# A hybrid encoder's mixer: the convolution's passes at a step's end, a norm factor on GpSimd, and squares between the parts of the head

## The chip, the cores and the metric

The kernel runs on one core of one Trainium2 chip. The metric is the time of the whole program on the device in microseconds (us), as the median of three runs. The engines are named as in the profile: PE is TensorE, DVE is VectorE, ACT is ScalarE, POOL is GpSimd and SP is SyncE, which only issues DMAs here.

## The reference

The input is x, 512 tokens of 1024 numbers. Each of two layers adds to x the output of a mixer and then of a mixture of experts. What matters here is the mixer, which is cut to its core (h is the normalised x):

```python
proj = rmsnorm(x, norm_mix[l]) @ w_in[l]
q, k, v, gate_b, gate_c, u = split(proj)             # 512, 128, 128, 512, 512, 512 wide
y_attn = windowed_gqa_with_sink(rope(q), rope(k), v, sink)   # 8 heads of 64, |i - j| <= 128
cu = gate_c * u
y_conv = gate_b * (cu[t-1] * w[0] + cu[t] * w[1] + cu[t+1] * w[2])
y = concat([rmsnorm(y_attn, g_attn), rmsnorm(y_conv, g_conv)])
x = x + y @ w_out[l]
```

Because the norm of x has one factor r per token, the projections can be made of x times the norm's weights alone, and r is multiplied in behind. The product gate_c * u then needs r squared for each token. The product with gate_b gets its one r within the norm of y_conv.

## The kernel before, in words

A mixer has three parts. In the **head**, 512 tokens of x are transposed on TensorE (parts T), copied out of PSUM as a high part by ACT and a low part by DVE (parts H), multiplied by the norm's weights. Every projection is made of high and low parts, three matmuls for each, so that the result is as exact as f32. The strings `HEAD` (layer 0) and `HEAD1` (layer 1) are the order of the head's parts, read by `stage`: f brings the end of the layer before, w splits a weight chunk, P makes a projection. Behind the head come **steps**. In step n a projection of 128 channels by 512 tokens is made on TensorE (8 parts, P in the string `STEP`), and the result of step n - 1 is taken over by `take`; FT lists whose projection it is: k, v, q (four pairs of heads), u, c (gate_c) and b (gate_b), of which the last three come four times each, and a u is followed by a c and the c by a b of the same 128 channels. Between the projection's parts the attention of a unit (one pair of heads and one block of 128 queries) is worked on:

```python
STEP = "P P K P S s T0 e T1 t1 n P R t0 w P P V v P P"
```

S is the scores on TensorE, s (`greatest`, L653) the maximum on DVE, e (`exps`) the exponentials on ACT, n (`normalise`, L671 to L674) the sum, the reciprocal and the scaling on DVE. T and t transpose the probabilities and split them (L410 on ACT, L411 on DVE), V and v multiply by the values. K calls `take`, R runs what is queued in `pend`, w splits the next weight chunk (L410, L411), and `post` runs at the end of the step. The last part are the **output** groups: y is split (L413 on ACT, L414 on DVE), multiplied by w_out, which GpSimd splits (`osplit`), and each result is added to x on DVE (L815) which frees its bank.

The names around the change: `rsv` holds the mean of squares per token, its rstd and the square of the rstd, in three rows. `sq_row` is r squared as a row of 512 tokens, the same in all partitions. In `take`, u is copied out of PSUM by ACT (L575), and multiplied by sq_row on DVE (L577); a c step multiplies the PSUM projection by u on DVE (L583), scales it by the middle weight on ACT (L584), and adds the two shifted terms in two passes on DVE (L585, L586). A b step multiplies that by its projection (L589), and `sums` adds up squares on ACT and GpSimd. `squares` (L481) is called at R of step 1 and makes the sums of squares of x by four ACT instructions, followed by the power on GpSimd.

What sets the order on each engine: TensorE and GpSimd are in program order (PINNED is "TG"). In the steps, DVE and ACT instructions are put in order when the program is built, by a planner's estimates of when each can start; in the head all three compute orders are those of the program. Tiles named t_N come from pools, and N is a count.

## Time and profile before

| What | us |
|---|---|
| median of three runs | 1368.87 |
| the three runs | 1370.92, 1368.45, 1368.87 |
| the profiled execution, its time | 1370.96 |
| the profiled execution, its span | 1369.2 |
| TensorE busy in the span | 1308.7 (96%) |
| DVE busy | 613.1 (45%) |
| ACT busy | 375.3 (27%) |
| POOL busy | 110.2 (8%) |

The time of an execution is from its start to its end as the device counts it, and the span is from the first to the last instruction in the trace. Busy shares are means over all stages. The mixers take 0 to 205 and 670 to 880 us; the experts lie between and behind them.

### The profile page before, as it was taken

Reading aid. Unit: us, or ns where it says so; the run is one execution under the profiler, and the core shown is the slowest. Engines: PE = TensorE matmul, PEld = TensorE weight load, DVE = VectorE, ACT = ScalarE, POOL = GpSimd, SP = SyncE. Lnnn points to the kernel's source line nnn. Section 1 sums busy time; section 2 is a strip of 40 time slices with the busy share of each in tenths; the row PEclk is TensorE's granted clock in tenths of the full one; section 3 lists DMA queues with packets and bytes.
Section 4 is the critical chain, followed back from the end, with each engine's and each line's share of the span. In section 5 each row is a group of like instructions: output and inputs, shape, how many; then the busy total and the mean of one; then the engine's idle time right before and its main releaser. Section 6 shows DMA issues by size and latency. Waiting matters only on the chain. (4 is left out here: it accounts for less than half of the span.)

```text
span 1369.2 us, 22469 instructions
## 1 busy us (share of the span) xinstructions
PE 1308.7 (96%) x8036; PEld 770.8 (56%) x8036; DVE 613.1 (45%) x1519; ACT 375.3 (27%) x819; POOL 110.2 (8%) x119
## 2 busy tenths in 40 slices
PE   9999899999999999999989998999999999999997
PEld 8777787445444355444377886865444443544442
DVE  4888745232344224222268888352334442332232
ACT  5565531221111111111156665212311011111112
POOL 1201340000000000000030023300000000000001
PEclk9999899999999999999999999999999999999999
DMA  8622267899999999999891223788999999999996
GB/s 257 189 65 75 93 261 278 344 377 419 419 418 419 419 419 419 418 419 419 329 280 50 67 75 130 263 329 343 378 418 419 419 418 419 419 419 419 418 418 253
DMA packets 160853, 438.47 MB, mean 320 GB/s; under 512 B 19352, under 2 KB 56672, under 8 KB 160736
## 3 DMA queue, kind: packets, MB, share of 16 engines
q1 hardware_dynamic: 160736, 436.98, 81.9%
q8 instruction: 65, 1.06, 0.3%
q14 instruction: 52, 0.43, 0.1%
HBM read 434.83 MB, written 2.10 MB: 319 GB/s over the span
## 5 line engine op out<-in xcount | busy, mean ns | idle before, releaser
L180 PE MATMUL A<-t,t 128*32 128x512 f32 (+3 forms) x3832 | 692.0, 527 | 12.3 <-DMA t<-in_w_expert_up_dram 2.5
L180 PEld LDWEIGHTS A<-t,t 128*32 128x32 f32 (+2 forms) x3832 | 334.4, 142 | 326.6 <-issue 235.9
L180 PE MATMUL C<-t,t 128*32 128x512 f32 (+4 forms) x1448 | 227.1, 569 | 4.0 <-DVE t L552 2.3
L180 PEld LDWEIGHTS C<-t,t 128*32 128x32 f32 (+2 forms) x1448 | 83.8, 126 | 132.0 <-issue 112.8
L414 DVE SCALAR_TENSOR_TENSOR t<-C,tg,t 128x512 fp32r<-128x512 f32 x56 | 41.3, 749 | 195.9 <-ACT t L413 194.5
L180 PE MATMUL B<-t,t 128*128 128x256 f32 (+3 forms) x836 | 112.0, 284 | 6.8 <-DVE t L1238 4.7
L1313 DVE SCALAR_TENSOR_TENSOR t<-A,tg,t 128x512 f32<-128x512 f32 x28 | 21.0, 751 | 213.6 <-PE A L180 197.1
L180 PEld LDWEIGHTS B<-t,t 128*128 128x128 f32 (+1 forms) x836 | 103.7, 186 | 22.5 <-issue 9.2
L180 PE MATMUL D<-t,t 128*128 128x512 f32 (+1 forms) x374 | 99.8, 366 | 10.9 <-DVE x L1344 6.3
L1344 DVE TENSOR_TENSOR x<-x,D 128x512 f32<-128x512 f32 x104 | 71.2, 685 | 77.6 <-PE D L180 77.3
L1312 ACT ACTIVATE t<-A,tg 128x512 f32<-128x512 f32 x28 | 19.3, 688 | 301.8 <-PE A L180 279.8
L413 ACT ACTIVATE t<-C,tg 128x512 fp32r<-128x512 f32 x56 | 37.8, 687 | 194.3 <-PE C L180 194.3
L180 POOL TENSOR_TENSOR t<-t,t 128x512 f32<-128x512 f32 (+1 forms) x34 | 61.2, 1801 | 213.1 <-ACT t L602 86.8
L1253 ACT ACTIVATE t<-B,gf 128x256 f32<-128x256 f32 (+1 forms) x96 | 38.4, 454 | 140.9 <-PE B L180 125.0
L180 PEld LDWEIGHTS D<-t,t 128*128 128x128 f32 x374 | 54.2, 179 | 39.7 <-DVE x L1344 13.1
L180 PE MATMUL F<-t,t 128*128 128x512 f32 x214 | 71.6, 414 | 0.1
L1344 DVE TENSOR_TENSOR x<-x,F 128x512 f32<-128x512 f32 x104 | 70.7, 680 | 0.0
L180 PE MATMUL B<-cst,t 128*128 128x128 f32 (+1 forms) x332 | 49.6, 274 | 14.0 <-DVE t L674 10.5
L180 PEld LDWEIGHTS B<-cst,t 128*128 128x128 f32 (+1 forms) x332 | 41.3, 151 | 24.7 <-issue 18.4
L180 PEld LDWEIGHTS F<-t,t 128*128 128x128 f32 x214 | 37.1, 188 | 18.9 <-DVE x L1344 11.4
L410 ACT ACTIVATE t<-t 128x1024 fp32r<-128x1024 f32 x44 | 45.8, 1054 | 0.1
L1215 DVE TENSOR_SCALAR t<-cst,sq 128x256 fp32r<-128x256 f32 (+1 forms) x64 | 17.2, 332 | 59.7 <-PE A L180 45.1
(278 smaller groups left out, 1059.2 us busy)
## 6 DMA issues: line engine op xcount, KB each, us to landing
t<-in_w_expert_gate_dram SPq DMA_DIRECT2D x256, 512.0 KB, 9.9
t<-in_w_expert_up_dram SPq DMA_DIRECT2D x256, 512.0 KB, 9.9
t<-in_w_expert_down_dram SPq DMA_DIRECT2D x256, 512.0 KB, 9.9
t<-in_w_in_dram SPq DMA_DIRECT2D x36, 512.0 KB, 6.4
t<-in_w_out_dram SPq DMA_DIRECT2D x16, 512.0 KB, 3.7
x<-in_x_dram SPq DMA_DIRECT2D x4, 512.0 KB
out_dram<-t SPq DMA_DIRECT2D x3, 512.0 KB, 2.7
t<-in_consts_dram SPq DMA_DIRECT2D x2, 512.0 KB
```

What stands on the lines that cost most here:

```text
L180: return (lambda *args, **kw: self.tc.keep_in_program_order(fn(*args, **kw))) if self.pinned else fn
L410: A.activation(hi, src, AF.Copy)
L413: A.activation(hi, src, AF.Copy, scale=scale)
L414: V.scalar_tensor_tensor(lo, src, scale, f(hi), op0=OP.mult, op1=OP.subtract)
L1215: V.tensor_scalar(oh[:, t, :w], io, sq[:, 0, t:t + 1], None, op0=OP.is_equal)
L1253: A.activation(hg[b][c // 4][:, c % 4 + cc, :w], p[:, cc, :w], AF.Copy, scale=g_ffn[:, c + cc:c + cc + 1])
L1312: A.activation(a, pg, AF.Silu, scale=rs)
L1313: V.scalar_tensor_tensor(a, pu, rs, a, op0=OP.mult, op1=OP.mult)
L1344: V.tensor_add(x[:, t, s], x[:, t, s], p)
```

## The change

Three things are moved. The four squares of x become stages c0 to c3 of the head, written between its parts, with a fresh junk tile for each; c3 also issues the power and the square of the rstd. The multiplication by `sq_row` leaves u (L577) and becomes a GpSimd instruction on the product of c and u, between DVE's product and ACT's scaling. And the two passes on DVE go into `post`, which runs at the end of the step.

```diff
--- before.py
+++ after.py
@@ -155,10 +155,10 @@
 PINNED = "TG"
 
 
-HEAD = ("z40 T00 T01 T02 T03 z08 T10 H00 T11 H01 T12 w0 H02 T13 H03 w1 z16 P00 T20 T30 H10 T21 T31 H11 T22 T32 H12 T23 T33 "
-        "H13 P01 P10 P11")
-HEAD1 = ("f0 f1 f2 w0 T00 T10 H00 T01 T11 H01 f3 T02 T12 H02 T03 T13 H03 w1 P00 T20 T30 H10 T21 T31 H11 P10 "
-         "T22 T32 H12 T23 T33 H13 P01 P11")
+HEAD = ("z40 T00 T01 T02 T03 z08 T10 H00 T11 H01 T12 w0 H02 T13 H03 w1 c0 c1 z16 P00 T20 T30 H10 T21 T31 H11 T22 T32 H12 T23 T33 "
+        "H13 c2 c3 P01 P10 P11")
+HEAD1 = ("f0 f1 f2 w0 T00 T10 H00 T01 T11 H01 f3 T02 T12 H02 T03 T13 H03 w1 c0 P00 T20 T30 H10 c1 T21 T31 H11 c2 P10 "
+         "T22 T32 H12 c3 T23 T33 H13 P01 P11")
 TURNS = ["BBCCDFBB", "BBBBCCBB"]
 
 AHEAD = [2, 3]
@@ -470,17 +470,15 @@
                 if a not in pp:
                     pp[a] = ps("A")
                 proj(a, pp[a], 0, ND, slice(b * 256, b * 256 + 256))
+            elif what == "c":
+                A.activation(t2([P, D], BF16), x[:, a], AF.Square, scale=D ** -0.5, accum_out=rsv[:, 0, a:a + 1])
+                if a == NT - 1:
+                    rstd_of(rsv[:, 0], rsv[:, 1])
+                    GP.tensor_mul(rsv[:, 2], rsv[:, 1], rsv[:, 1])
             else:
                 z = ps("D", (P, P))
                 for _ in range(10 * a + b):
                     T.matmul(z, onesb, onesb, start=True, stop=True)
-
-        def squares():
-            junk = t2([P, D], BF16)
-            for t in range(NT):
-                A.activation(junk, x[:, t], AF.Square, scale=D ** -0.5, accum_out=rsv[:, 0, t:t + 1])
-            rstd_of(rsv[:, 0], rsv[:, 1])
-            GP.tensor_mul(rsv[:, 2], rsv[:, 1], rsv[:, 1])
 
         for what in (HEAD, HEAD1)[l].split():
             stage(what[0], int(what[1]), int((what + "0")[2]))
@@ -573,17 +571,16 @@
             elif what[0] == "u":
                 st["u"] = t2([P, S])
                 A.activation(st["u"], p, AF.Copy)
-                u = st["u"]
-                post.append(lambda: V.tensor_mul(u, u, sq_row))
             elif what[0] == "c":
                 cu = t4([P, S + 2])
                 GP.memset(cu[:, 0:1], 0.0)
                 GP.memset(cu[:, S + 1:S + 2], 0.0)
                 c, v = what[1], st["u"]
                 V.tensor_mul(cu[:, 1:S + 1], p, v)
+                GP.tensor_mul(cu[:, 1:S + 1], cu[:, 1:S + 1], sq_row)
                 A.activation(v, cu[:, 1:S + 1], AF.Copy, scale=cw[:, 1, c:c + 1])
-                V.scalar_tensor_tensor(v, cu[:, 0:S], cw[:, 0, c:c + 1], v, op0=OP.mult, op1=OP.add)
-                V.scalar_tensor_tensor(v, cu[:, 2:S + 2], cw[:, 2, c:c + 1], v, op0=OP.mult, op1=OP.add)
+                post.append(lambda: [V.scalar_tensor_tensor(v, cu[:, n:S + n], cw[:, n, c:c + 1], v, op0=OP.mult, op1=OP.add)
+                                     for n in (0, 2)])
             else:
                 c = what[1]
                 V.tensor_mul(yc[c // 2][:, c % 2], p, st["u"])
@@ -731,8 +728,6 @@
                 elif m == "R" and n == 2:
 
                     flush(2)
-                elif m == "R" and n == 1:
-                    squares()
                 elif m == "w":
                     ahead()
                 elif m in "Ssen" and a:
```

The order of VectorE (DVE) in layer 0's first u step, from the sum of the denominators (L671 before, L668 of the changed kernel) to the maximum of the next unit (L653, L650, the rows ISA). t_858 is u, t_91 holds the mask and sq_row, nb the denominators, t_777 and t_780 the probabilities; before:

```order
L671 TENSOR_TENSOR nb<-nb 128x2
L710 TENSOR_TENSOR t_412<-D,yl 64x128
L577 TENSOR_TENSOR t_858<-t_858,t_91 128x512
L672 RECIPROCAL nb<-nb 128x2
L710 TENSOR_TENSOR t_412<-D,yl 64x128
L653 ISA t_864,nb<-C,t_91,sink 128x256
L653 ISA nb 128x1
L674 TENSOR_SCALAR t_777<-t_777,nb 128x256 x2
L653 ISA t_864,nb<-C,t_91,sink 128x256
```

and of the changed kernel:

```order
L668 TENSOR_TENSOR nb<-nb 128x2
L707 TENSOR_TENSOR t_423<-D,yl 64x128
L669 RECIPROCAL nb<-nb 128x2
L671 TENSOR_SCALAR t_780<-t_780,nb 128x256 x2
L707 TENSOR_TENSOR t_423<-D,yl 64x128
L650 ISA t_867,nb<-C,t_91,sink 128x256
L650 ISA nb 128x1
```

The product L577 is gone, and the normalisation (L674, now L671) stands ahead of both maxima and not between them.

The order of ScalarE (ACT) at the end of the head of layer 1; the rows with rsv are squares of x, those with gx are the copies out of the transposes, and t_6205 and t_6219 are split weights; before:

```order
L180 ACTIVATE t_5979<-B,gx 128x256 x2
L180 ACTIVATE t_5980<-B,gx 128x256 x2
L180 ACTIVATE t_6205<-t_5925 128x1024
L528 ACTIVATE t_6211<-A 128x512
L481 ACTIVATE t_6214,rsv<-x 128x1024 x2
L569 ACTIVATE t_6235<-A 128x512
L481 ACTIVATE t_6214,rsv<-x 128x1024 x2
L180 ACTIVATE t_6222<-t_5935 128x1024
```

and of the changed kernel:

```order
L180 ACTIVATE t_6065,rsv<-x 128x1024
L180 ACTIVATE t_5980<-C,gx 128x256 x2
L180 ACTIVATE t_6101,rsv<-x 128x1024
L180 ACTIVATE t_5981<-C,gx 128x256 x2
L180 ACTIVATE t_6112,rsv<-x 128x1024
L180 ACTIVATE t_5982<-B,gx 128x256 x2
L180 ACTIVATE t_6148,rsv<-x 128x1024
L180 ACTIVATE t_5983<-B,gx 128x256 x2
L180 ACTIVATE t_6219<-t_5928 128x1024
L526 ACTIVATE t_6225<-A 128x512
L180 ACTIVATE t_6228<-t_5938 128x1024
L567 ACTIVATE t_6241<-A 128x512
```

The squares stood behind the copies, around the projections' copies (L528, L569), and now one stands ahead of each pair of copies.

The order of VectorE (DVE) in the step of layer 0's fourth c, from the product of c and u (L583 before, L579 of the changed kernel; t_1508 and t_1511 are u and then the sum of the passes) to the splits of the gated product (L414); before:

```order
L583 TENSOR_TENSOR t_1586<-A,t_1508 128x512
L653 ISA t_1597,nb<-C,t_91,sink 128x384
L653 ISA nb 128x1
L585 SCALAR_TENSOR_TENSOR t_1508<-t_1586,prm,t_1508 128x512
L653 ISA t_1597,nb<-C,t_91,sink 128x384
L653 ISA nb 128x1
L411 TENSOR_TENSOR t_1609<-B,t_1608 128x256 x2
L586 SCALAR_TENSOR_TENSOR t_1508<-t_1586,prm,t_1508 128x512
L655 TENSOR_SCALAR nb<-nb 128x2
L414 SCALAR_TENSOR_TENSOR t_1643<-t_410,prm,t_1642 128x512
```

and of the changed kernel:

```order
L579 TENSOR_TENSOR t_1588<-A,t_1511 128x512
L650 ISA t_1598,nb<-C,t_91,sink 128x384
L650 ISA nb 128x1
L650 ISA t_1598,nb<-C,t_91,sink 128x384
L650 ISA nb 128x1
L411 TENSOR_TENSOR t_1610<-B,t_1609 128x256
L652 TENSOR_SCALAR nb<-nb 128x2
L411 TENSOR_TENSOR t_1610<-B,t_1609 128x256
L653 TENSOR_TENSOR nb<-sink,nb 128x2
L582 SCALAR_TENSOR_TENSOR t_1511<-t_1588,prm,t_1511 128x512 x2
L668 TENSOR_TENSOR nb<-nb 128x2
L586 TENSOR_TENSOR t_422<-A,t_1511 128x512
```

The two passes (L585 and L586, now two rows L582) stood apart from each other between the maxima, and now stand together behind the splits of B (L411).

## Rows read from the trace of the kernel before

**Rows 1.** The page's line of busy time, share of the span and instructions, and the trace's windows over the two mixers: length in us, then busy us of PE, PEld, DVE, ACT and POOL (with instructions), granted clock, DMA share and GB/s.

```profile
PE 1308.7 (96%) x8036; PEld 770.8 (56%) x8036; DVE 613.1 (45%) x1519; ACT 375.3 (27%) x819; POOL 110.2 (8%) x119
...
0.00:205.00 205.00, 191.45 (x1031) 161.97 (x1032) 146.44 (x362) 108.75 (x249) 48.31 (x45) 0.98 0.48 157
...
670.00:880.00 210.00, 194.39 (x1043) 156.96 (x1043) 147.31 (x355) 111.34 (x252) 51.01 (x42) 0.99 0.45 147
```

**Rows 2.** TensorE's timeline at the passes behind the normalisation of the three u steps of layer 0 and of the first two of layer 1. Columns here and in the groups of timelines below: start us, us, engine, line, operation, out<-in, shape, count, and in brackets idle time before and its releaser.

```profile
73.97 0.67 PE L180 MATMUL B<-cst,t 128*128 128x128 f32 x4 [1.09 <-DVE t L674]
...
105.11 0.67 PE L180 MATMUL B<-cst,t 128*128 128x128 f32 x4 [1.13 <-DVE t L674]
...
135.38 0.67 PE L180 MATMUL B<-cst,t 128*128 128x128 f32 x4 [1.14 <-DVE t L674]
...
750.78 0.67 PE L180 MATMUL B<-cst,t 128*128 128x128 f32 x4 [1.10 <-DVE t L674]
...
781.22 0.68 PE L180 MATMUL B<-cst,t 128*128 128x128 f32 x4 [1.09 <-DVE t L674]
```

**Rows 3.** VectorE's timeline in layer 0's first u step.

```profile
71.97 0.67 DVE L577 TENSOR_TENSOR t<-t,t 128x512 f32<-128x512 f32 x1
...
73.07 0.48 DVE L653 CUSTOM_DVE_ANT_0 t<-C,t,sink 128x256 f32<-128x256 f32 x1
...
73.48 0.61 DVE L674 TENSOR_SCALAR t<-t,nb 128x256 f32<-128x256 f32 x2
```

**Rows 4.** The timeline of GpSimd, VectorE and TensorE where the first query's rotation ends, in layer 0 and then in layer 1.

```profile
38.51 1.27 POOL L180 TENSOR_TENSOR t<-t,t 128x512 f32<-128x512 f32 x1
...
39.54 0.78 DVE L577 TENSOR_TENSOR t<-t,t 128x512 f32<-128x512 f32 x1
...
42.45 0.47 PE L180 MATMUL C<-t,t 128*128 128x256 f32 x2 [0.37 <-DVE t L552]
...
715.95 1.29 POOL L180 TENSOR_TENSOR t<-t,t 128x512 f32<-128x512 f32 x1
...
716.76 1.02 DVE L577 TENSOR_TENSOR t<-t,t 128x512 f32<-128x512 f32 x1 [0.90 <-ACT t L575]
...
719.92 0.47 PE L180 MATMUL C<-t,t 128*128 128x256 f32 x2 [1.60 <-DVE t L552]
```

**Rows 5.** The head of layer 1: TensorE's wait, ScalarE's last copies out of the transposes, the last square, and GpSimd's power.

```profile
705.66 0.82 PE L180 MATMUL C<-cst,rsv 128*128 128x128 f32 x5 [1.60 <-POOL rsv L180]
...
695.16 0.84 ACT L180 ACTIVATE t<-B,gx 128x256 fp32r<-128x256 f32 x2 [2.78 <-PE B L180]
...
703.01 1.06 ACT L481 ACTIVATE t<-x 128x1024 bf16<-128x1024 f32 x1
...
704.56 1.04 POOL L180 TENSOR_TENSOR rsv<-rsv,mhalf 128x4 f32<-128x4 f32 x1
```

**Rows 6.** ScalarE's timeline in the head of layer 0, the copies out of the transposes behind its idle time.

```profile
15.29 0.84 ACT L180 ACTIVATE t<-D,gx 128x256 fp32r<-128x256 f32 x2 [2.00 <-PE D L180]
```

**Rows 7.** Layer 0's first c step: ScalarE's scaling, VectorE's first pass and its splits of B, TensorE's wait for them.

```profile
49.51 0.72 ACT L584 ACTIVATE t<-t,prm 128x512 f32<-128x512 f32 x1 [1.68 <-DVE t L583]
...
50.33 0.75 DVE L585 SCALAR_TENSOR_TENSOR t<-t,prm,t 128x512 f32<-128x512 f32 x1 [0.86 <-ACT t L584]
...
52.74 0.75 DVE L411 TENSOR_TENSOR t<-B,t 128x256 fp32r<-128x256 f32 x2
...
53.54 0.57 PE L180 MATMUL D<-t,t 128*64 128x256 f32 x3 [1.17 <-DVE t L411]
```

**Rows 8.** VectorE's and GpSimd's timelines, instructions of these two engines beside each other and apart.

```profile
56.65 0.75 DVE L674 TENSOR_SCALAR t<-t,nb 128x384 f32<-128x384 f32 x2
...
86.84 1.83 DVE L674 TENSOR_SCALAR t<-t,nb 128x384 f32<-128x384 f32 x2
...
87.17 1.29 POOL L180 TENSOR_TENSOR t<-t,t 128x512 f32<-128x512 f32 x1 [16.61 <-ACT t L602]
...
64.56 1.79 POOL L180 TENSOR_TENSOR t<-t,t 128x512 f32<-128x512 f32 x1 [24.72 <-DVE t L531]
...
142.76 0.61 DVE L653 CUSTOM_DVE_ANT_0 t<-C,t,sink 128x384 f32<-128x384 f32 x1
...
142.94 1.30 POOL L180 TENSOR_TENSOR t<-t,t 128x512 f32<-128x512 f32 x1 [2.04 <-ACT t L602]
```

**Rows 9.** VectorE's and GpSimd's timelines in the last steps of layer 0's mixer, and TensorE's wait in the same place of layer 1.

```profile
138.53 2.38 DVE L671 TENSOR_TENSOR nb<-nb 128x2 f32<-128x2 f32 x1 [1.46 <-ACT nb L665]
...
142.16 0.69 DVE L583 TENSOR_TENSOR t<-A,t 128x512 f32<-128x512 f32 x1
...
145.32 2.39 POOL L180 TENSOR_TENSOR t<-t,t 128x1024 fp32r<-128x1024 f32 x1 [1.02 <-ACT t L410]
...
146.18 2.07 DVE L586 SCALAR_TENSOR_TENSOR t<-t,prm,t 128x512 f32<-128x512 f32 x1
...
148.25 0.74 DVE L414 SCALAR_TENSOR_TENSOR t<-t,prm,t 128x512 fp32r<-128x512 f32 x1
...
162.41 0.75 DVE L815 SCALAR_TENSOR_TENSOR x<-A,rr,x 128x512 f32<-128x512 f32 x1
...
838.97 0.96 PE L180 MATMUL A<-t,t 128*128 128x512 f32 x3 [1.82 <-DVE x L815]
```

**Rows 10.** The trace's window at the end of layer 0's mixer, columns as in the windows above; the clock is the number ahead of the last two.

```profile
154.00:164.00 10.00, 9.58 (x32) 7.86 (x31) 8.18 (x20) 3.87 (x10) 3.37 (x2) 0.50 0.05 11
```

## The prediction

> **What bounds the kernel now.** I read the page first: TensorE is busy for 1308.7 of 1369.2 us [rows 1], so all that any change of order can win is the other 60.5 us. The windows then say where these lie. Tokens mix in two stretches, 0 to 205 and 670 to 880 us, in which TensorE is busy 191.45 and 194.39 us: 29.2 us idle, half of all, while VectorE is busy 146 and 147, ScalarE 109 and 111, GpSimd 48 and 51 [rows 1]. The change touches the mixers alone. No engine is full there, and the DMA share is below a half, so what sets the time is chains: TensorE's short waits, each with its releaser. I took those from TensorE's timeline, and for each the VectorE, ScalarE and GpSimd rows just ahead. A mixer's end moves all that follows rigidly, so a wait won on TensorE is a wait won at the end, unless the next one gives it back.
>
> **The u steps (the multiplication by the squared factor leaves VectorE).** The product of u with the factor, 128x512, takes 0.67 us, and stands between the sum of the denominators and their reciprocal; a 0.48 us maximum stands ahead of the normalisation too [rows 3]. TensorE waits for exactly that normalisation: 1.09 and 1.13 us in layer 0, 1.10 and 1.09 in layer 1 [rows 2]. In the new order the normalisation comes directly behind the reciprocal and one 0.28 us addition. Up to 0.67 + 0.48 + 0.08 = 1.23 us come off, more than each wait: the waits go whole, 1.09 + 1.13 + 1.10 + 1.09 = **4.4 us**. Bounds: 2.7 if only the 0.67 comes off in each, 4.4 if all. I take 4.4, since both instructions are gone from ahead. Late next are the B copies and their splits; the timeline has no wait of TensorE at them in these steps, so nothing is charged. The third u step (1.14 [rows 2]) I take with the end.
>
> **The start of the scores.** The first u's product ran 39.54 to 40.32 and 716.76 to 717.78, right ahead of the rotation's addition; the addition's other input comes from GpSimd at 39.78 and 717.24 [rows 4]. So 0.54 us each can go, and TensorE waits at 719.92 for what follows [rows 4]. Layer 0's wait there, at 42.45, is 0.37 [rows 4]. I take 0.4 each: **0.8** (bounds 0 to 1.1).
>
> **The heads (squares moved between the head's splits).** In layer 1 the last two squares ran to 704.07, then GpSimd's power, and TensorE stood 1.60 us until 705.66 for it [rows 5]. With the squares earlier that wait vanishes. Against it: the fourth square, 1.05 us and its 0.19 accumulator read, now stands in front of the last copies out of the transposes, which start at 695.16 after 2.78 us of waiting for TensorE [rows 5]; the square ends later than the transposes by about 1 us, and the first projection's last two chunks wait some 0.6. Net **1.0** (bounds 0.5 to 1.6). In layer 0 no wait of TensorE has GpSimd's power as its releaser, so nothing is won. Two squares (2 x 1.25) go into a 2.00 us hole ahead of the copies at 15.29 [rows 6], which come 0.25 later: a loss of **0.25** (bounds 0 to 0.5); the other two lie behind the last copies.
>
> **The c steps (one GpSimd instruction put in the chain, two passes put last).** Gone from VectorE's middle: two passes of 0.75. New: GpSimd multiplies the product by the factor, 1.29 us by the nearest GpSimd row of that shape alone, 1.79 where a VectorE instruction runs beside it [rows 8]. The chain is VectorE's product, GpSimd's, then ScalarE's scaling, which started at 49.51 as soon as the first was done [rows 7] and now starts at 50.85 (1.29 and a hop of 0.05 later). Behind it on VectorE waits the first pass, and behind that the low parts of B's split; behind it on ScalarE wait the copies of B, on which the values and the first pass depend. In layer 0's first c step the copies end at 52.15, the first pass at 52.3, and the low parts, which started at 52.74 behind both passes, end at 53.2, if nothing blocks, where TensorE was released at 53.54 [rows 7]. That makes bounds of a gain of 0.3 and a loss of 0.5, with GpSimd at 1.79; I take a loss of 0.1. In layer 1 the normalisation comes behind VectorE's product and is blocked by GpSimd's, as in rows 8 below: a loss of 0.6 (0 to 1.0). In the second c steps the scale also stands ahead of the copies of B: 0.15 each, 0.3 (bounds 0 to 1.2). In the third, the copies' weight split comes ahead: 0.05 for both. Together a loss of **1.05**.
>
> A conflict of two engines weighs against the change, and decides its sign. The normalisation takes 0.75 us alone, and 1.83 at 86.84, when GpSimd's product ran from 87.17 to 88.46: it ended 0.2 us behind that one's end [rows 8]. A four-element addition took 2.38 us at 138.53, beside GpSimd's 1024-wide subtraction [rows 9]. VectorE's maximum, 384 wide and with one operand in PSUM, took 0.61 at 142.76 although GpSimd's addition ran from 142.94 [rows 8]; 256 wide it takes 0.48 [rows 3], so 0.61 is no more than its size. So GpSimd's eight new products can each hold back one VectorE instruction by up to 1.08 us. The Trainium skill has this as a rule (SBUF — State Buffer, section "Who interferes with whom"): VectorE and GpSimd share a port pair as an exclusive lock, and a VectorE instruction with two SBUF inputs, or in one of the faster modes, is shut out by a GpSimd instruction that reads SBUF; with a PSUM operand it isn't. The trace agrees with both halves, 1.83 against 0.75 and 0.61 beside GpSimd. The page alone would leave all eight steps open to a block, which is the second rival. I charge it once, for layer 1's first c step, since in the others the two VectorE instructions behind the product are the maxima, with one operand in PSUM.
>
> **The end.** In layer 0's last steps the chain before is: addition 138.53 blocked to 140.91; the product of the fourth c at 142.16; pass two at 146.18, blocked to 148.25 by GpSimd's split that began at 145.32; the splits of the gated product from 148.25, and TensorE's group behind them; the update of x at 162.41 that frees the bank for the third output group [rows 9]. In the new order the third u's wait (1.14) goes, and the fourth c's product comes some 1.3 us earlier. GpSimd then runs the sums' addition and the factor's product (2 x 1.29), the scale follows at 143.5, the two passes stand behind GpSimd's split and end at 147.4 or so, the b product at 148.2, and the first gated split at 149.05, where it was 148.99 for the second piece: most of the 2.3 us won at 135 to 142 is given back in a wait there. What stays is the block at 146.18 (2.07 rather than 0.75 [rows 8, 9]), and with it the second half's lag: the third output group at 162.25 rather than 164.5 by my count, **2.2** (bounds 0.5 to 3.6). In layer 1 the same wait was 1.82 at 838.97 [rows 9] with less of a block ahead, and I take **0.6** (a loss of 1.5 to a gain of 2.0). Together 2.8.
>
> **Sum.** 4.4 + 0.8 + 1.0 - 0.25 - 1.05 + 2.8 = 7.7 us. Against the profiled execution of 1370.96 us (span 1369.2; 1.8 lie around it) that is 1363.3. That execution is 2.1 us above the median of the three runs, 1368.87, so the median forecast is **1361.2**. Edits costed at nothing: the extra memory tiles of the squares, and the orders of TensorE and SyncE, which are as before.
>
> **Rivals.**
> First, **no change**: the mixer's steps have VectorE at 146.44 of 205 [rows 1], and a wait won in a u step returns at the next c step, whose chain is now longer by GpSimd's 1.29 and hop. For it: each u step is followed by a c step. Against: TensorE's work fills the mixers but for short waits, and an earlier u step gives the next step's VectorE, ScalarE and GpSimd work an earlier start too. Only the heads' 0.5 or so would be left: 1368.4.
> Second, **slower, by the block**: GpSimd's product shuts VectorE out in every c step, not one. Each then costs 1.08 (1.83 - 0.75 [rows 8]) plus the chain's 0.75 (1.29 + about 0.2 of hops less the 0.75 of the pass that leaves): 1.8, for eight 14.6, against gains of 4.4 + 0.8 + 1.0 + 2.3 - 0.25 = 8.25: 6.3 slower, 1375.2. It decides from 8.25 / 8 = 1.03 us in a c step. For it: 1.83 at 86.84. Against: what stands behind the product are the maxima, and the passes are last now.
> Third, **a larger gain**: TensorE ran 154 to 164 us at a granted clock of 0.50, the lower level, 1.2 GHz [rows 10], after the waits of the end of layer 0. If the earlier end takes these waits away, and the clock stays at 2.4 GHz, ten us at half speed hold five more: 1361.2 - 5.0 = 1356.2.
>
> **Chances.** Forecast 0.60 (1357.5 to 1366), larger gain 0.10, no change 0.18, slower 0.12. A change below 0.2%, 2.7 us, is not told from none here. So faster 0.70, same 0.18, slower 0.12. The range goes from 1357.0 to 1370.0: the larger gain's further part and the slower case lie outside, 2 in 10 together; it takes in no change.
>
> **What would show it.** Right: TensorE's waits behind the normalisation at 74, 105, 751 and 781 gone; none for the power at 705; GpSimd's products at 1.29 to 1.8; TensorE idle in the mixers down by about 5. Wrong: VectorE instructions of over 1.5 us at the c steps, a wait on ScalarE's scale in most of them, or a wait of 3 us before the output groups; then the second rival is at work.

## The result and the profile after

The changed kernel takes 1357.76 us (median of four runs, 1357.31 to 1358.57) where the kernel before, run beside it, takes 1369.62: a ratio of 0.9914, 95% interval 0.9897 to 0.9931, or 11.9 us less. The forecast was 7.7 us less, 1361.2 in a range of 1357.0 to 1370.0. The direction and the range held; the size was too small by a third.

The page's busy line of the changed kernel, and its windows over the mixers (columns as in [rows 1]; the second mixer begins some 5 us earlier, and its window is taken 10 us earlier):

```profile
PE 1306.3 (96%) x8036; PEld 774.0 (57%) x8036; DVE 609.6 (45%) x1511; ACT 374.3 (28%) x819; POOL 119.2 (9%) x127
```

```profile
0.00:205.00 205.00, 194.21 (x1065) 165.41 (x1066) 146.76 (x367) 110.33 (x253) 53.97 (x51) 0.98 0.50 161
...
660.00:870.00 210.00, 199.10 (x1063) 161.10 (x1060) 148.06 (x358) 111.67 (x253) 55.26 (x46) 0.98 0.46 156
```

VectorE has eight instructions less, GpSimd eight more, each as in the diff. A fixed window takes in other work once a mixer is shorter, so its busy times are no measure of what was won. Over the whole span TensorE's idle time, span less busy time, falls from 60.5 to 50.0 us. Where that was won can be read from TensorE's order: it runs the same 8036 matmuls in the same order in both kernels, so the start of the k-th can be compared with the start of the k-th. The table does so at the places of the prediction (difference of the two starts, us, worked out from the two traces; negative is earlier):

| place, time before | first mixer | second mixer |
|---|---|---|
| ahead of the head's projections (19, 698) | +0.49 | -4.81 |
| the norm's matmuls in the second (706) | | -6.45 |
| k and first q done (43, 720) | +0.10 | -6.94 |
| first c step (54, 730) | -0.27 | -6.95 |
| first u step (74, 751) | -1.49 | -8.18 |
| second u step (105, 781) | -2.92 | -9.50 |
| third u step (135, 812) | -4.25 | -10.89 |
| ahead of the output groups (146, 822) | -5.45 | -12.08 |
| in them (158, 835) | -3.09 | -9.32 |
| third output group (164.5, 844) | -4.76 | -11.50 |
| experts, behind the wait for their weights (470, 1146) | -5.67 | -13.09 |

The u steps first. This is VectorE's timeline of the changed kernel at the place of [rows 3], and TensorE's there and in the second u step:

```profile
71.46 0.15 DVE L668 TENSOR_TENSOR nb<-nb 128x2 f32<-128x2 f32 x1
71.53 0.28 DVE L707 TENSOR_TENSOR t<-D,yl 64x128 f32<-64x128 f32 x1
71.73 0.15 DVE L669 RECIPROCAL nb<-nb 128x2 f32<-128x2 f32 x1
71.92 0.62 DVE L671 TENSOR_SCALAR t<-t,nb 128x256 f32<-128x256 f32 x2
```

```profile
72.00 0.64 PE L180 MATMUL C<-t,t 128*128 128x256 f32 x4
72.48 0.61 PE L180 MATMUL B<-cst,t 128*128 128x128 f32 x4
...
102.19 0.67 PE L180 MATMUL B<-cst,t 128*128 128x128 f32 x4
```

The normalisation starts 0.46 us behind the sum, where it was 1.78 behind ([rows 3], with the sum at 71.70), and the transposes follow TensorE's work ahead of them with no wait in brackets. The five waits of [rows 2] are gone, and the sixth of their kind, 1.16 at 811.50 in the kernel before.

In the first c step of layer 0, VectorE, GpSimd and ScalarE:

```profile
48.89 0.69 DVE L579 TENSOR_TENSOR t<-A,t 128x512 f32<-128x512 f32 x1
...
51.73 0.75 DVE L582 SCALAR_TENSOR_TENSOR t<-t,prm,t 128x512 f32<-128x512 f32 x1 [1.02 <-ACT t L581]
52.40 0.42 DVE L411 TENSOR_TENSOR t<-B,t 128x256 fp32r<-128x256 f32 x1
...
52.80 0.42 DVE L411 TENSOR_TENSOR t<-B,t 128x256 fp32r<-128x256 f32 x1
```

```profile
49.65 1.29 POOL L180 TENSOR_TENSOR t<-t,t 128x512 f32<-128x512 f32 x1 [9.29 <-DVE t L579]
```

```profile
50.98 0.72 ACT L581 ACTIVATE t<-t,prm 128x512 f32<-128x512 f32 x1 [3.05 <-POOL t L180]
51.60 0.64 ACT L410 ACTIVATE t<-B 128x256 fp32r<-128x256 f32 x2
```

The scale is 1.5 us later than in [rows 7], and the low parts of B all the same are done 0.27 earlier, because one pass and not two stands ahead of them. TensorE's wait there, 1.17 in [rows 7], is 0.60. GpSimd's eight new products take 1.28 to 1.31 each. Three of them block VectorE. One does so in layer 1's first c step, as the prediction had it (VectorE, GpSimd and TensorE):

```profile
719.25 1.62 DVE L671 TENSOR_SCALAR t<-t,nb 128x256 f32<-128x256 f32 x2
```

```profile
719.41 1.31 POOL L180 TENSOR_TENSOR t<-t,t 128x512 f32<-128x512 f32 x1 [8.62 <-DVE t L579]
```

```profile
720.93 0.44 PE L180 MATMUL B<-cst,t 128*128 128x128 f32 x2 [0.44 <-DVE t L671]
```

The two others are the products of the fourth c steps, at 139.00 and 808.48. Each holds an instruction of two columns, which takes 0.16 us in the first c step, for 0.82 and 0.81; in layer 0:

```profile
139.50 0.82 DVE L652 TENSOR_SCALAR nb<-nb 128x2 f32<-128x2 f32 x1
```

The end of the mixer is what is left to win. TensorE's timeline in layer 0, and VectorE's and GpSimd's ahead of it:

```profile
143.73 0.73 PE L180 MATMUL A<-t,t 128*128 128x512 f32 x2 [0.96 <-ACT t L413]
145.85 0.96 PE L180 MATMUL A<-t,t 128*128 128x512 f32 x3 [1.39 <-DVE t L414]
148.19 2.07 PE L180 MATMUL A<-t,t 128*128 128x512 f32 x4 [1.38 <-DVE t L414]
159.74 2.33 PE L180 MATMUL A<-t,t 128*128 128x512 f32 x9 [1.14 <-DVE x L810]
```

```profile
140.57 2.25 DVE L653 TENSOR_TENSOR nb<-sink,nb 128x2 f32<-128x2 f32 x1
142.75 1.53 DVE L582 SCALAR_TENSOR_TENSOR t<-t,prm,t 128x512 f32<-128x512 f32 x2
```

```profile
137.70 1.29 POOL L180 TENSOR_TENSOR t<-t,t 128x512 f32<-128x512 f32 x1 [2.06 <-ACT t L599]
...
139.00 3.81 POOL L180 TENSOR_TENSOR t<-t,t 128x512 f32<-128x512 f32 x2
```

GpSimd has the sums' addition, the factor and the split of the output weights in one row (the last row shown holds the factor and, from 140.40, the split of 2.41), and an addition of two columns on VectorE takes 2.25 beside the split; 58 of this trace's 64 additions of that shape take 0.14 to 0.16 us, and the six others each run beside a 1024-wide subtraction on GpSimd. The passes, the product with gate_b and its splits queue behind it: 3.7 us of waiting, and then TensorE at half clock:

```profile
146.00:154.00 8.00, 6.62 (x22) 5.37 (x22) 7.54 (x15) 3.48 (x7) 1.26 (x1) 0.59 0.10 40
```

In the kernel before the half clock lay at 154 to 164 [rows 10], behind a longer wait for a normalisation:

```profile
153.58 1.37 PE L180 MATMUL B<-cst,t 128*128 128x128 f32 x6 [1.90 <-DVE t L674]
```

That wait is gone, as is the same one at 829.69 in layer 1. So the half clock has moved, and is shorter. The waits are no shorter in sum: in this stretch of layer 0 the kernel before has 0.97, 0.29, 1.90 and 0.42, or 3.6.

### The profile page after: what moved, and what is told of

Read it like the earlier page. It is cut to its first block, busy times and chain, and to the rows that moved or that the text cites. A ratio compares the mean times of both kernels' runs of the same rounds, so it can differ in the third digit from the quotient of the medians.

```text
span 1356.3 us, 22449 instructions
## 1 busy us (share of the span) xinstructions
PE 1306.3 (96%) x8036; PEld 774.0 (57%) x8036; DVE 609.6 (45%) x1511; ACT 374.3 (28%) x819; POOL 119.2 (9%) x127
## 3 DMA queue, kind: packets, MB, share of 16 engines
q8 instruction: 65, 1.06, 0.3%
## 5 line engine op out<-in xcount | busy, mean ns | idle before, releaser
L414 DVE SCALAR_TENSOR_TENSOR t<-C,tg,t 128x512 fp32r<-128x512 f32 x56 | 41.4, 749 | 195.9 <-ACT t L413 194.4
L180 PE MATMUL B<-t,t 128*128 128x256 f32 (+3 forms) x836 | 115.1, 289 | 6.9 <-DVE t L1233 4.8
L180 PEld LDWEIGHTS B<-t,t 128*128 128x128 f32 (+1 forms) x836 | 106.7, 192 | 22.5 <-issue 9.2
L180 POOL TENSOR_TENSOR t<-t,t 128x512 f32<-128x512 f32 (+1 forms) x42 | 71.0, 1692 | 199.0 <-ACT t L599 59.5
L1206 POOL TENSOR_SCALAR sq<-rv 128x8 f32<-128x8 f32 x16 | 3.9, 248 | 495.2 <-DVE t L1211 460.1
```

Of the source, the lines that this page charges most:

```text
L180: return (lambda *args, **kw: self.tc.keep_in_program_order(fn(*args, **kw))) if self.pinned else fn
L414: V.scalar_tensor_tensor(lo, src, scale, f(hi), op0=OP.mult, op1=OP.subtract)
L1206: GP.tensor_scalar(sq, q["v"][:, 16:18, :], -float(b * P), None, op0=OP.add)
```

## Experiments: which part gives the gain

Three kernels each put one part of the change back, a fourth puts GpSimd's factor at VectorE's old place. The edits, against the changed kernel; the first has the heads of before and `squares()` at R of step 1:

```diff
 u1: the strings HEAD and HEAD1 of before, and
+                elif m == "R" and n == 1:
+                    squares()
 u2:
+                u = st["u"]
+                post.append(lambda: V.tensor_mul(u, u, sq_row))
...
-                GP.tensor_mul(cu[:, 1:S + 1], cu[:, 1:S + 1], sq_row)
 u3:
-                post.append(lambda: [V.scalar_tensor_tensor(v, cu[:, n:S + n], cw[:, n, c:c + 1], v, op0=OP.mult, op1=OP.add)
-                                     for n in (0, 2)])
+                V.scalar_tensor_tensor(v, cu[:, 0:S], cw[:, 0, c:c + 1], v, op0=OP.mult, op1=OP.add)
+                V.scalar_tensor_tensor(v, cu[:, 2:S + 2], cw[:, 2, c:c + 1], v, op0=OP.mult, op1=OP.add)
 u4: as u2, with
+                post.append(lambda: GP.tensor_mul(u, u, sq_row))
```

**Squares back.** 

> The changed kernel with the squares of x back at R of step 1, after the head; the factor on GpSimd and the late passes stay. Theory (each wait that went is worth its own length): the wait for GpSimd's power in layer 1's head returns, 1.6 us, and the 0.7 that the squares cost in front of the last copies goes, so 0.9 slower than the changed kernel, about 1358.7; in layer 0 the head comes 0.5 earlier again, because the half-clock stretch at 12 to 14 us belongs to the squares. Rival (the early squares give an early factor, and that is what frees the steps): 4 us or more slower, 1362. Rival (the half clock in layer 0's head is chance): layer 0's head as in the changed kernel.

**Factor back.** 

> The changed kernel with the factor back on u on VectorE, at the end of the u step; squares early and passes late stay. Theory: the waits of TensorE behind the normalisation in the six u steps return in part or whole (1.1 each, 6.6 together) and the starts of the scores lose 0.9; the c steps' scale is early again and gives 0.5 to 1 back: 5 to 7 slower than the changed kernel, 1363 to 1365. Rival (the late passes alone made the u steps free, since they pull the queue of VectorE forward): within 1 us of the changed kernel, 1357 to 1359.

**Passes back.** 

> The changed kernel with the two passes back in program order behind the scale, where the planner puts them between the maxima; squares early and the factor on GpSimd stay. Theory: with the factor's 1.29 us in the chain the passes wait on VectorE's queue, and the splits of B behind them come 0.5 to 1 us late in the first three c steps of each layer; the waits of the u steps stay gone: 3 to 6 slower than the changed kernel, 1361 to 1364, with TensorE's waits behind L411 in the c steps. Rival (the place of the passes does not matter, the planner hides them): 1357 to 1359.

**Factor on u, but on GpSimd.** 

> The changed kernel with GpSimd's multiplication on u at the end of the u step rather than on the product in the c step, so that the factor is out of VectorE and out of the c chain too. Theory: GpSimd's 1.29 us now runs beside the normalisation of the u step, which has two forms of block (up to 1.08 us each in six u steps where TensorE waits for exactly that): 1 to 4 slower than the changed kernel, 1359 to 1362. Rival (what counts is that VectorE is relieved, and a chain shorter by 1.29 in the c steps is a gain): 1 to 2 faster, 1356.

**The factor alone, in the kernel before** (its edit is u2's, the other way round). 

> The kernel before with one part of the change alone: the factor leaves u on VectorE and becomes GpSimd's instruction on the product; squares after the head and passes in place as before. Theory after the first four runs (with the factor back on u the whole gain is gone, with the squares or the passes back nothing is): this part gives all of it, 1357 to 1359. Rival (two parts each suffice only together with the factor): 1361 to 1365.

| kernel | median us | ratio to before | 95% interval |
|---|---|---|---|
| the changed kernel | 1357.76 | 0.9914 | 0.9897 to 0.9931 |
| squares back | 1357.57 | 0.9919 | 0.9906 to 0.9933 |
| factor back | 1368.69 | 0.9999 | 0.9990 to 1.0008 |
| passes back | 1358.11 | 0.9917 | 0.9904 to 0.9931 |
| factor on u, GpSimd | 1363.45 | 0.9962 | 0.9949 to 0.9976 |
| factor alone | 1357.85 | 0.9914 | 0.9896 to 0.9932 |

The factor's move gives the whole gain: without it nothing is left (10.9 us lost, where I had expected 5 to 7), and alone it gives all. The late passes are worth nothing that can be measured, against what I had expected of them here (3 to 6 us with the passes back): with them in place TensorE's wait in the first c step is 0.59, as with them late. With the factor back, the waits of the kernel before stand again, here in TensorE's timeline (three of the six):

```profile
74.99 0.67 PE L180 MATMUL B<-cst,t 128*128 128x128 f32 x4 [1.10 <-DVE t L672]
...
106.12 0.67 PE L180 MATMUL B<-cst,t 128*128 128x128 f32 x4 [1.15 <-DVE t L672]
...
136.40 0.67 PE L180 MATMUL B<-cst,t 128*128 128x128 f32 x4 [1.14 <-DVE t L672]
```

The squares are worth what the prediction said in their place, and not in the time. With them back, TensorE's row in layer 1's head is again

```profile
699.07 1.16 PE L180 MATMUL C<-cst,rsv 128*128 128x128 f32 x8 [1.60 <-POOL rsv L180]
```

and by the table's measure the changed kernel wins 0.9 there, which this kernel does not. But this kernel is not slower in the median. Its half clock at the end of layer 0 is shorter (a granted clock of 0.79 in the window 146 to 154, where the changed kernel has 0.59), and by the table's measure it is 0.85 ahead there. In layer 0's head the same kernel runs at half clock too, although its squares are elsewhere, and the kernel with the factor alone does not. The window 11 to 16 us, first with the squares back, then the factor alone:

```profile
11.00:16.00 5.00, 4.64 (x26) 4.64 (x27) 1.87 (x5) 1.56 (x3) 2.31 (x1) 0.66 1.11 372
```

```profile
11.00:16.00 5.00, 4.50 (x39) 4.50 (x39) 2.26 (x6) 2.83 (x7) 1.76 (x1) 1.00 1.12 371
```

So the half clock there is no cost of the squares: it is there with late squares, and four of the profiled executions with early squares are without it. By the table's measure it costs 1.5 us between 11 and 16 us in each of the eight executions that have it. The squares have a price of their own, though. In those four executions TensorE waits just behind, for the late copies and their low parts on VectorE: 0.21 in the kernel with the idle product (below), 0.44 with the factor on u on GpSimd, 0.49 and, in two waits, 0.72 in the two kernels with both edits at the mixers' ends (below). This is the second of these:

```profile
16.76 11.75 PE L180 MATMUL A<-t,t 128*128 128x256 f32 x83 [0.44 <-DVE t L180]
```

Between 15 and 19 us these four lose 0.2 to 1.0 by the table's measure, the factor alone nothing, and the kernels at half clock nothing either. So the early squares cost layer 0's head 0.2 to 1.0 us where the clock stays up, and nothing that can be seen where it falls. What makes the clock fall there in some kernels' profiled executions and not in others was not found.

The factor on u on GpSimd loses half the gain, a little more than the 1 to 4 us expected, and most of that by the block that the prediction feared for the c steps. GpSimd's and VectorE's timelines of that kernel in the first u step of layer 0, and TensorE's wait:

```profile
72.37 1.31 POOL L180 TENSOR_TENSOR t<-t,t 128x512 f32<-128x512 f32 x1 [5.27 <-ACT t L573]
```

```profile
72.46 1.25 DVE L669 TENSOR_TENSOR nb<-nb 128x2 f32<-128x2 f32 x1
```

```profile
74.51 0.67 PE L180 MATMUL B<-cst,t 128*128 128x128 f32 x4 [0.87 <-DVE t L672]
```

The addition of the denominators, 0.15 us when alone, is held 1.1 longer, and the normalisation is late again. The same stands in layer 1, and at both starts of the scores the rotation's addition is held in the same way, with waits of TensorE of 1.03 and 2.23 where the changed kernel has none and 1.19. That is 3.8 of the 5.7 us lost; the second and third u steps are free of waits. Of the rest, 0.6 is a longer wait in layer 0's first c step (1.17), and in layer 1 TensorE runs at half clock for a while behind the wait of 2.23 (a granted clock of 0.77 from 714 to 718 us). The rule of the Trainium skill (SBUF — State Buffer, section "Who interferes with whom") says that a VectorE instruction with both inputs in SBUF is shut out while GpSimd reads SBUF; this row, 1.25 us for two columns, agrees: it ends at 73.71, GpSimd's product at 73.68.

## Experiments: place, load or dependence

The factor's move did three things at once: VectorE has less to do, the u step's chain is free of it, and the c step's product no longer waits for it. Two kernels tell these apart:

```diff
 v1: 
-                GP.tensor_mul(cu[:, 1:S + 1], cu[:, 1:S + 1], sq_row)
+                V.tensor_mul(cu[:, 1:S + 1], cu[:, 1:S + 1], sq_row)
 d1:
+                u, idle = st["u"], t2([P, S])
+                post.append(lambda: V.tensor_mul(idle, u, sq_row))
```

**The factor on the product, on VectorE.** 

> The changed kernel with the factor on the product in the c step as in the change, but on VectorE rather than GpSimd: VectorE does as much as in the kernel before, at another place, and GpSimd has none of the eight new instructions. Theory (what counts is that the factor left the chain from the sum to the normalisation in the u step): the six waits behind the normalisation stay gone and the scale comes 0.6 earlier, with no block: as fast as the changed kernel or up to 3 us faster, 1355 to 1359. Rival (what counts is that VectorE was relieved of eight times 0.67 us): the waits come back in the c steps, 0.6 each, 1361 to 1364.

It took 1356.98 us, a ratio of 0.9904 (0.9887 to 0.9921). VectorE is as busy as before the change (613.1 in [rows 1]), as this kernel's page says:

```profile
PE 1304.4 (96%) x8036; PEld 769.7 (57%) x8036; DVE 612.7 (45%) x1519; ACT 375.1 (28%) x819; POOL 115.7 (9%) x119
```

The gain is all there, so the load is not it.

**An idle product at the old place.** 

> The changed kernel with one VectorE instruction more in each u step: the product of u and the factor, at the place in the order that it had in the kernel before, written to a tile that nobody reads; all else is the changed kernel's, GpSimd's factor included. Theory (the 0.7 us at this place hold back the normalisation, which TensorE waits for): the waits of 1.1 behind the normalisation return and with them the time of before, 1366 to 1370. Rival (what cost was that the c step's product waited for the factor in u): nothing returns, 1357 to 1360.

It took 1362.33 us, a ratio of 0.9953 (0.9936 to 0.9969): between the theory and the rival. The trace says why, and more clearly than either. The planner, which orders VectorE, put the idle product at its old place at the start of the scores (39.63) and in the first u step of each layer, and behind the c's product in the two other u steps, since nothing needs it. In layer 0's first u step, VectorE's rows and TensorE's wait are those of the kernel before:

```profile
71.69 0.67 DVE L575 TENSOR_TENSOR t<-t,t 128x512 f32<-128x512 f32 x1
72.29 0.15 DVE L671 RECIPROCAL nb<-nb 128x2 f32<-128x2 f32 x1
...
102.80 0.14 DVE L671 RECIPROCAL nb<-nb 128x2 f32<-128x2 f32 x1
102.98 0.62 DVE L673 TENSOR_SCALAR t<-t,nb 128x256 f32<-128x256 f32 x2
...
109.10 0.68 DVE L575 TENSOR_TENSOR t<-t,t 128x512 f32<-128x512 f32 x1
```

```profile
73.69 0.56 PE L180 MATMUL B<-cst,t 128*128 128x128 f32 x3 [1.09 <-DVE t L673]
...
103.51 0.64 PE L180 MATMUL B<-cst,t 128*128 128x128 f32 x4
```

1.09 us where it stands in the chain, none where it stands behind. It is the place, shown within one kernel, and not the dependence, since no c step of this kernel waits for the idle product. By the table's measure the first u steps give nothing here (-0.28 to -0.28, and -5.60 to -5.59), the second ones 1.32 and 1.23. Two waits of 1.09 and two starts of the scores (about 0.45 each) are 3.1 of the 4.6 us by which this kernel is slower than the changed one (5.3 by the two ratios); what makes up the rest stays open.

## Experiments: the end of the mixers

What is left is the wait ahead of the output groups. Two suspects, GpSimd's queue of three and its split's block, were taken away alone and together; in each the text gives the edit against the changed kernel:

```diff
 h1, in a c step:
-                GP.tensor_mul(cu[:, 1:S + 1], cu[:, 1:S + 1], sq_row)
+                (V if c == 3 else GP).tensor_mul(cu[:, 1:S + 1], cu[:, 1:S + 1], sq_row)
...
+                if c == 3:
+                    post.pop()()
 h2, in osplit:
-            split(live["out", l, kh, n, kk], None, hi, lo, GP)
+            split(live["out", l, kh, n, kk], None, hi, lo, V if (kh, n, kk) in OSPLIT[1:3] else GP)
 h3: h1 and h2
 w1: v1 and h2
 s1: w1 with u1
```

**The last c on VectorE.** 

> The changed kernel with the factor of the fourth c of each layer on VectorE, and that step's two passes directly behind the scale. Theory (the wait of 0.96, 1.39 and 1.38 ahead of the output groups comes from GpSimd's queue there: sums, factor, split, the last of which blocks a VectorE addition for 2.25): the factor's part of it goes, the scale comes 1.3 earlier and the passes run ahead of the split, so 1 to 3 us a layer: 1352 to 1356. Rival (the block of the addition sets the wait, and it only moves by the 1.3 that GpSimd's split comes earlier, while VectorE gets 0.7 more): 1356 to 1359.

**Two output weight splits on VectorE.** 

> The changed kernel with the second and third split of the output weights (the subtraction 1024 wide) on VectorE rather than GpSimd, 1.2 us on VectorE where it took GpSimd 2.4. Theory (GpSimd's split blocks VectorE's addition at 140.6 for 2.25 us, behind which the last exponential's queue on ScalarE and the gated product's split wait, and TensorE for these; and the update of rr at 156.6 for 2.34): the blocks go, VectorE pays 1.2 for each, so 1 to 2 us a layer: 1354 to 1356. Rival (VectorE is the bound of this stretch and pays as much as it wins): 1357 to 1360.

**Both.** 

> The changed kernel with the fourth c's factor on VectorE, that step's passes directly behind the scale, and the second and third split of the output weights on VectorE; the other six factors stay on GpSimd. Theory: as the kernel with all factors on VectorE and those splits, within 1 us (the first three c steps of a layer are free of blocks but one), 1352 to 1355. Rival (VectorE gets too much in the last c step, 0.7 + 1.5 + 1.2 ahead of the gated splits): 1355 to 1358.

**All factors and two splits on VectorE.** 

> The changed kernel with the factor on the product on VectorE in all eight c steps, and the second and third split of the output weights on VectorE: no GpSimd instruction beside the chain of the last c any more. Theory (the two edits act at different waits: the scale's start, and the blocked additions): their gains add up in part, 1352 to 1354.5. Rival (both shorten the same stretch ahead of the output groups, whose later wait for the update of x takes it back): as the splits alone, 1354 to 1356.5.

**The same with the squares back.** 

> The kernel with all eight factors on VectorE's product and two output weight splits on VectorE, with the squares of x back after the head; passes late. Theory (the squares are worth the wait in layer 1's head, 1.6, less 0.7 ahead of it): 0.9 slower than with the early squares, 1351 to 1352, and no more is lost where no later wait absorbs it. Rival (what the head wins is absorbed at the expert stage's wait for weights, as the first run suggests): as with the early squares, 1350 to 1350.7.

| kernel | median us | ratio to before | 95% interval |
|---|---|---|---|
| last c on VectorE | 1356.54 | 0.9899 | 0.9882 to 0.9915 |
| two splits on VectorE | 1354.71 | 0.9894 | 0.9878 to 0.9911 |
| both | 1350.05 | 0.9862 | 0.9845 to 0.9878 |
| all factors and two splits on VectorE | 1350.39 | 0.9863 | 0.9846 to 0.9879 |
| the same, squares back | 1350.91 | 0.9867 | 0.9850 to 0.9883 |

Each alone wins 1 to 3 us, near what can be told from the changed kernel; the first of the two lands in its rival's range. Together they win 7.7, clear of noise and more than I expected (1352 at best). The gains of each alone add up to 4.3 (4.8 by the ratios, against 7.1 together), but each ratio has an interval of 2.3 us either way, so the times alone do not show that both win more than their sum. TensorE's and VectorE's timelines with both show what went:

```profile
145.14 1.42 PE L180 MATMUL A<-t,t 128*128 128x512 f32 x4 [0.30 <-DVE t L414]
149.25 1.05 PE L180 MATMUL F<-onesf,t 128*128 128x1 f32 x8 [0.50 <-POOL t L180]
155.20 2.32 PE L180 MATMUL A<-t,t 128*128 128x512 f32 x9 [1.29 <-DVE x L812]
```

```profile
141.87 0.16 DVE L655 TENSOR_TENSOR nb<-sink,nb 128x2 f32<-128x2 f32 x1
141.94 1.22 DVE L411 TENSOR_TENSOR t<-t,t 128x1024 fp32r<-128x1024 f32 x1
```

```profile
145.00:160.00 15.00, 13.06 (x69) 10.29 (x70) 13.30 (x40) 7.72 (x20) 5.04 (x2) 1.00 0.22 72
```

The addition is back at 0.16 us, the split costs VectorE 1.22 where it cost GpSimd 2.4 and VectorE a block of 2.25, the waits of 3.7 are 0.30 and a new one of 0.50, and the clock stays at the upper level over the whole stretch (the last row is the trace's window). In the changed kernel it fell after waits of 0.96, 1.39 and 1.38 between 143 and 148. Here, and with all factors and two splits on VectorE, it did not.

The two edits help each other, as the wait ahead of the third output group shows; in layer 0, first with the last c on VectorE, then with the two splits on VectorE:

```profile
157.08 3.49 PE L180 MATMUL A<-t,t 128*128 128x512 f32 x9 [2.35 <-DVE x L812]
```

```profile
158.34 2.33 PE L180 MATMUL A<-t,t 128*128 128x512 f32 x9 [1.59 <-DVE x L810]
```

It is 1.14 in the changed kernel, and 1.29 with both. With the last c alone on VectorE the waits ahead of it fall from 3.73 to 1.84, but GpSimd's third split still holds VectorE's update of rr (2.31 us at 153.93, as 2.34 at 156.56 in the changed kernel), and 1.2 us comes back as this wait. With the splits alone the waits ahead fall to 2.27, with the factor on GpSimd still in the chain. With both they are 0.80. TensorE's waits in this stretch, this one included and both layers added, are 9.75 us in the changed kernel, 8.38 and 7.97 with one edit and 4.17 with both. So both together take away 5.58 us of waits, where the two alone add up to 3.15; that the clock gives the rest of the 7.7 is argued, not shown. The squares, taken back in the best kernel, cost 0.5 us in the median, which these intervals don't tell from nothing. In the trace the 1.60 us wait in layer 1's head is there again.

## Why the prediction held, and where it was short

- **The u steps, 4.4.** Right in mechanism: the product's place in the chain, and the first two waits of each layer went whole. By the table the four steps won 1.22, 1.43, 1.23 and 1.32, together 5.2: somewhat more than the waits themselves.
- **The starts of the scores, 0.8.** 0.39 and 0.49: right.
- **The heads, 1.0 and -0.25.** 0.92 in layer 1, from ahead of the delayed copies to behind the norm's matmuls: right in the trace, though the median does not show it. In layer 0 the squares did delay the copies as described, by 0.2 to 1.0 where the clock stayed up, which goes beyond the bound of 0.5; in the changed kernel's own execution the 0.49 is the net of two stretches at half clock, one in each kernel, and not the squares.
- **The c steps, a loss of 1.05.** This step failed in its size, and its sign. Layer 0's first c step won 0.37, a little beyond the better of the two bounds (a gain of 0.3) that the prediction worked out from the rows and then did not take; layer 1's lost 0.6 to the block and had it back by the low parts of B. The second and third steps lost nothing. Together some 0.4 won, 1.4 off the forecast. What was overlooked: the waiting scale delays the copies of B, but the low parts then stand behind fewer VectorE instructions; in the kernel with the passes in place the planner gets to the same 0.59.
- **The end, 2.8.** 1.84 in layer 0 (forecast 2.2) and 2.0 in layer 1 (forecast 0.6), from the second u step to the third output group. The give-back was as described, waits of 3.7 ahead of the output groups. What the prediction left out is the 1.90 us that TensorE waited for a normalisation at 153.58 and 829.69, which went in both layers. But the block by GpSimd's split did not go as expected; it fell on another VectorE instruction (2.25 at 140.57 where it was 2.07 at 146.18 [rows 9]). Layer 1 was under-sized because I took the two layers' ends to differ; in the new order they are alike to 0.2 us.
- **What the sum did not have.** Behind the mixers the changed kernel gains another 0.9 and 1.6 by the table, at TensorE's waits for expert weights. The kernel with the factor back, which is no faster than before, has 1.1 and 1.3 of the same there. So that part is most likely of the profiled execution of the kernel before (1370.96 us, 1.3 above the later median) and not of the change; what sets the weights' pace there stays open.
- **The rivals.** The conflict of GpSimd and VectorE was real, in three c steps of eight (by 1.0 in one and 0.66 in two) and at the mixers' ends, and the kernel with the factor on u on GpSimd shows it at the price forecast, 1.1 per block. The prediction charged one. In the fourth c steps it overlooked that the splits of B, and an instruction of two columns between them, now follow the maxima while GpSimd's product still runs; in the five others nothing is held, and what VectorE runs beside the product there reads PSUM: the maxima, as argued, and in the third c steps a split of B. The larger gain by the clock did not come: the half clock moved from the waits at 153 to the waits at 148. In the kernels with both edits at the mixers' ends the two stretches are at the upper level.
- **The signs.** Those of being right came, with TensorE's idle time down by more than the 5 us. But so did one of being wrong: a wait of over 3 us before the output groups, 3.7 in three pieces, and with it a VectorE instruction of 2.25 us in a c step. The second rival did not follow from it, and the kernel is faster; the kernel before has waits of 3.6 in the same stretch, so this sign could not tell the two apart.

## What to carry to other kernels

An instruction on an engine that is half idle can be the whole cost, if it stands between a sum and the reciprocal that the busiest engine waits for: look at what stands in the chain, and move that, before counting load. Of a change in several parts, put each back by itself: here two of the three were worth nothing in the median. And work sent to GpSimd should be set where VectorE's next instructions read PSUM, as the maxima of 0.61 beside it did here; two-column additions were held as long as large ones.

## What the runs showed of the hardware

A VectorE addition of 128 x 2, two columns and not the four elements of the prediction, took 2.25 us beside GpSimd's 1024-wide subtraction and 1.25 beside its 512-wide product, where it takes 0.15 alone. Both ended with GpSimd's instruction, at 142.82 against 142.81 and at 73.71 against 73.68: what is left of that instruction sets the length of the block, and not the size of what is blocked. The subtraction takes VectorE 1.22 us and GpSimd 2.4, so for VectorE it was cheaper to do the work itself than to be held by it. And the granted clock fell to the lower level in the first 16 us in the changed kernel and in the one with the squares back (0.67 and 0.66 in the window 11 to 16) and not in the one with the factor alone (1.00), after TensorE waits there of 1.06 and 0.76 in all three; the runs do not say why. That stretch costs 1.5 us in each execution that has it.
